# Strassen trunk on one core: weight blocks of 2 to 4, sums of squares in PSUM, softmax scale on ScalarE, and biases and silus issued once their operand is written

## The chip, the core and the metric

One core of a Trainium2 chip runs the whole kernel as one program. The metric is device time in microseconds; the time before is the median of three runs. The profile is one further execution of the same program.

The engines are named as in the profile: PE is the matrix engine (PEld its weight loads), DVE the vector engine, ACT the scalar (activation) engine, POOL the GpSimd engine, and SP the engine that issues nearly all DMAs. In the traces of this kernel each engine takes its instructions in the order of the program, and one that waits for another engine's semaphore holds up what stands behind it.

## The reference

One inference step of a two-layer trunk on 640 tokens (128 context tokens, 512 latent tokens) with 2048 features, in float32. Each layer is: RMS norm with a modulation, one wide input projection, two mixers side by side, a SiLU gate, an output projection, and a gated residual add.

```
even layer:  windowed attention with sinks   ||  gated linear attention (GLA)
odd layer:   neighbourhood attention (8 heads) ||  spatial gating (gMLP)
y = concat(mixer1, mixer2) * silu(gate)        # gate: part of the input projection
x = x + G * (y @ w_out)                        # G: gated residual, one per token group
final: rms_norm(x)
```

The modulation has its own matrix-vector products (the `ada` weights). The outputs are the tokens of both groups and the keys, values and states for the caches.

## The kernel before, in words

**Matmuls.** Activations lie in SBUF with features on the partitions and the 640 tokens along the free axis, in two halves of 320 (`HT`). A float32 product is made of three fast products: each operand is split into a high part, rounded to `fp32r`, and a low part, the rest. Of `high*high + high*low + low*high` each 128 x 128 weight block costs three matmuls of 320 columns (322 where two more columns carry the bias of the modulation's shift). Activations are `acth` and `actl`, weights are `whi` and `wlo`.

**Weight blocks.** A weight is loaded from DRAM by SP, ACT copies it to `whi` (a rounding copy), and POOL subtracts, `wlo = raw - whi`. Both go into a ring of 2560 columns (`RING`), that is 20 blocks of 128. In the plain products a split takes 4 blocks (512 columns) at once. A PE product frees its block in the ring (`wdone`) when the last matmul has been issued.

**Strassen pairs.** Most products of two output chunks c1, c2 with the two token halves go through `spair`: seven products instead of eight, called A11, A12, S1, S2, S4, S3, A22 for the weights that they use. Each product is made of 8 blocks (`ALL`, 31 such pairs) or 6 (`NS`, layer 0's output projection). A, the weight of the pair, has four quarters, called pieces 0 to 3 (A11, A12, A21, A22; quarters 0 to 2 in `rs`, quarter 3 in `adas`), and the sums S1 to S4 are made by four DVE instructions of 1024 columns, into piece 4 (`wraw`) or in place:

```
add1: wraw = q2 + q3     (S1)      add2: q2 = wraw - q0    (S2)
add3: q1 = q1 - q2       (S4)      add4: wraw = q3 - q2    (S3)
```

The activation sums that S1, S2 and A22 meet are `eh`/`el` (the first six blocks) and `fh`/`fl` (blocks 7 and 8). A split takes two blocks (256 columns), four splits a product, 28 a pair. The order of products is A11, A12, S1, S2, S4, S3, A22; in the first pair of a run of pairs A22 comes before S3. The next pair's quarters 0 and 1 are loaded after S4's splits, and quarters 2 and 3 at the end of the pair's list.

**The order of the work.** The program is written out by hand-made planning. The class `Pace` keeps a model of each engine's time; `tick` is called between matmuls (every second block) and issues, in program order, the work that the model takes to be due: the loads and splits of weights (`wpump`, which lets them run ahead by `lags`), the tasks of the mixers (generators that yield until an operand is ready), and a low-priority task for the `ada` products. What is issued early on an engine whose operand is late blocks that engine's queue.

**Evacuations.** When a projection's product is done, `lin` (projections) or `gate` (gates) brings it out of PSUM: DVE multiplies by the RMS factor `rstd` (PSUM to SBUF), ACT copies the two bias columns (`bc`), then ACT adds the bias (`lin`) or applies a silu with that bias (`gate`), and for most gates DVE multiplies the silu into the mixer's output `y`. All of these are issued in one go when PE's product has been issued. Where both halves come at once (`kpair`), DVE copies the bias and the multiplication is a task of its own (`late`). After it, `then` starts what depends on the result (a head, a transposition).

**Other places that the change touches.** `out_evac` makes the residual add of the output projection and the sums of squares for the next norm: ACT squares, then POOL (layer 0) or DVE (layer 1) adds to `ssq` in SBUF. `na_head` is a head of the neighbourhood attention: five blocks of scores, softmax (`soft1`, `soft2`), transposes, and products with the values `vk`; in the first and the last latent block one of the two value tiles has only 64 rows, and that matmul runs on half the partitions. `soft2` divides by the softmax sum, on ACT in the attention with sinks and on DVE in the neighbourhood attention.

Almost every operation is recorded through one helper, so line L218 stands for all of DVE, ACT and POOL, L447 for matmuls, L452 for transposes, and L484 for DMAs; the tile names tell them apart.

Of the kernel before, what the change touches and what calls it, by code (L numbers as in the profile page):

```python
# [35 lines left out]
NY, NZ, STAY = 8, 6, 10  # L36
OFF = 4
# [17 lines left out]
class Pace:  # L55
# [10 lines left out]
    COST = {"v": (0.07, 1 / 960), "a": (0.095, 0.84 / 1000), "g": (0.04, 2.35 / 1000)}  # L66
# [178 lines left out]
class Trunk:  # L245
# [9 lines left out]
    def __init__(self, tc, d, es):  # L255
# [6 lines left out]
        self.tasks = []  # L262
# [6 lines left out]
        self.cut = HT  # L269
# [37 lines left out]
        self.ident = self.P([128, 128], "ident")  # L307
# [94 lines left out]
    def widen(self, cs):  # L402

        yield from self.wait("r11", *(f"evac{c}" for c in cs))
        self.close_arena()
# [63 lines left out]
    rooms, calms, lags = (0.5, 1.5, 1.5), (3.0, 3.0), (3.0, 3.0, 2.0, 1.5, 1.0)  # L469
# [180 lines left out]
    def steps(self, c1, c2):  # L650

        names = lambda *x: [(c1, f) for f in x]
        if self.count[c1] == ALL:
            return names("A11", "A12", "S1", "S2", "S4", *(("A22", "S3") if c1 in self.opens else ("S3", "A22")))
        return [*names("A11"), (c1, PLAIN, 0), *names("A12", "S1", "S2", "S4"), (c2, PLAIN, 0), *names("S3", "A22")]

    def strassen_jobs(self, c1, c2, last, unit):
        ns, J = self.count[c1], self.jobs
        n, sub = 128 * ns, 2 if ns == ALL else ns // 2
# [10 lines left out]
        def load(i, c):  # L670
            if last is not None or ns != ALL:
                names = ()
            else:
                names = ("K", "H") if i else ("I", "J", "L")
            four = lambda x: x.rearrange("p (g r) c -> p g r c", r=4)
# [3 lines left out]
                    (piece(i + q, a, b), four(self.chunks[c][0])[:, JT[a] // 4 : JT[a] // 4 + (b - a) // 2, 2 * q : 2 * q + 2, :])  # L679
                    for q in range(2)  # L680
                    for a, b in ((0, 4), (4, ns))
                ],
                names,
# [3 lines left out]
        if last is None:  # L687
            J += [load(0, c1), load(2, c2)]
        else:
            J.insert(last[0], load(0, c1))  # L690
            J.insert(last[1] + 1, load(2, c2))
# [3 lines left out]
        if ns == ALL:  # L695
            after = {("A12", 3): [add1], ("S1", 1): [add2], ("S2", 1): [add3], ("S4", 1): [add4]}
        else:
            after = {("A12", 1): [add1, add2], ("S1", 1): [add3], ("S2", 1): [add4]}
        for c, f, *r in self.steps(c1, c2):
# [3 lines left out]
            for q in range(ns // sub):  # L703
                J.append(("split", (c1, f, q), lambda i=at[f], q=q: piece(i, sub * q, sub * q + sub), sub, 128, at[f] == 4))
                J += after.get((f, q), [])
            if f == "S4":
                done = len(J)
        return done, len(J)
# [27 lines left out]
    def wpump(self, force=False):  # L736
# [20 lines left out]
        lag = self.lags[min(sum(b - a for a, b in self.live.values()) // 512, 4)]  # L757
# [209 lines left out]
    def spair(self, c1, c2):  # L967
# [7 lines left out]
        sub = 2 if ns == ALL else ns // 2  # L975
# [31 lines left out]
        def product(b, view, f, x):  # L1007
            st = first(b)
            for i in range(ns):
                hi, lo = self.wget((c1, f, i // sub))  # L1010
                three(view(b), hi[:, i % sub, :], lo[:, i % sub, :], x(i), st and i == 0, i == ns - 1)
                if i % 2:
                    self.tick()
                if i % sub == sub - 1:
                    self.wdone((c1, f, i // sub))
# [239 lines left out]
    def lin(self, dst, scale=1.0, perm=False, then=None):  # L1255
# [3 lines left out]

        def evac(pa, pb):  # L1260
            M = dst.shape[0]
            lat = dst[:, NCTX:T].rearrange("p (g r c) -> p r g c", r=8, c=8) if perm else None
            if pa is not None:
                bc = box["bc"] = self.s("bc", 2)
# [7 lines left out]
                nc.scalar.activation(bc[:M], pa[:M, 0:2], AF.Copy, scale=scale)  # L1272
                nc.scalar.activation(dst[:, 0:NCTX], dst[:, 0:NCTX], AF.Identity, bias=bc[:M, 0:1], scale=scale)
            if pb is not None:
# [5 lines left out]
                nc.scalar.activation(dst[:, NCTX:T], dst[:, NCTX:T], AF.Identity, bias=bc[:M, 1:2], scale=scale)  # L1280
                if then:
                    then()

        return evac


    def gate(self, y, ring):
# [7 lines left out]
        def evac(pa, pb):  # L1295
# [9 lines left out]
            if pa is not None:  # L1305
                bc = box["bc"] = self.s("bc", 2)
                g = box["g"] = y if ring is None else ring.next()
                nc.vector.tensor_tensor(g[:, 0:HT], pa[:, 2 : 2 + HT], self.rstd[:, 0:HT], ALU.mult)
                nc.scalar.activation(bc, pa[:, 0:2], AF.Copy)
                self.act(g[:, 0:NCTX], g[:, 0:NCTX], AF.Silu, bias=bc[:, 0:1])  # L1310
                self.act(g[:, NCTX:HT], g[:, NCTX:HT], AF.Silu, bias=bc[:, 1:2])
                if ring:
                    nc.vector.tensor_tensor(y[:, 0:HT], y[:, 0:HT], g[:, 0:HT], ALU.mult)
            if pb is not None:
                bc, g = box["bc"], box["g"]
                nc.vector.tensor_tensor(g[:, HT:T], pb[:, 0:HT], self.rstd[:, HT:T], ALU.mult)
                self.act(g[:, HT:T], g[:, HT:T], AF.Silu, bias=bc[:, 1:2])
                if ring:
                    nc.vector.tensor_tensor(y[:, HT:T], y[:, HT:T], g[:, HT:T], ALU.mult)
# [1735 lines left out]
```

## Time and profile before

| | |
|---|---|
| median of three runs | 2063.18 us (2063.1 to 2065.52) |
| the profiled execution | 2068.56 us, its span 2066.8 us |
| mean granted clock of PE | 0.995 |
| PE busy | 2026.2 us, 98% of the span |
| DVE, ACT, POOL busy | 67%, 54%, 67% |
| DMA | 344.21 MB, mean 167 GB/s |

The stages by time, in us from the start of the span: 0 to 150 the first modulation and the first norm; 150 to 850 the even layer's projections with both mixers beside them; 850 to 1060 its gates' end and output projection; 1060 to 1310 the odd layer's gMLP projections; 1310 to 1650 the neighbourhood attention beside its projections; 1650 to 1850 the gates of the odd layer; 1850 to 2030 its output projection; then the final norm.

How to read it: a share of busy time says which engine could be the bound, not whether its stream has holes. Ends of matmuls are modelled in the profile, so a hole shorter than about a matmul's drain does not show as idle time. Counting matmuls in a window, and looking at starts, does show it. Timelines give the start, the length, the engine, the line and the operation, then the idle time in front and what ended it. Lines of groups give the count, the busy time, the mean of one in ns, and the idle time in front.

### The profile page before, as it was taken

How to read it: one execution, taken by the hardware profiler on the slowest of the kernel's cores; microseconds unless marked ns; L12 is line 12 of the kernel's file. 1: busy time of each engine (PE TensorE's matmuls, PEld its weight loads, DVE VectorE, ACT ScalarE, POOL GpSimd, SP SyncE). 2: the span in 40 equal slices, each digit the busy share in tenths (PEclk: the TensorE clock that was granted, in tenths of full speed). 3: DMA queues.
4: the chain of work that ended last, by engine and by line, in shares of the span. 5: the costliest groups of instructions: out<-in, count | busy, mean ns of one | idle time of the engine just before them, and what ended most of it. 6: DMA issues, size and time to landing. Idle time of an engine off the chain costs nothing.

```text
span 2066.8 us, 41426 instructions
## 1 busy us (share of the span) xinstructions
PE 2026.2 (98%) x14255; PEld 1978.7 (96%) x14255; DVE 1374.5 (67%) x3182; ACT 1109.7 (54%) x2758; POOL 1382.8 (67%) x1408
## 2 busy tenths in 40 slices
PE   8999999999999999999999999999999999999997
PEld 6899999999999999999999999999999999999996
DVE  4556678576667655888687777666676555577555
ACT  5445455444665565544565545555555655555543
POOL 4544455446455445888566978776866688968994
PEclk9999999999999999999999999999999999999999
DMA  9955433346466444677534344434434344265437
GB/s 382 393 200 162 128 111 106 120 128 206 142 205 209 148 156 155 198 241 221 204 127 133 121 155 151 128 118 138 142 115 132 99 154 131 85 211 184 141 102 280
DMA packets 234324, 344.21 MB, mean 167 GB/s; under 512 B 22048, under 2 KB 139648, under 8 KB 234112
## 3 DMA queue, kind: packets, MB, share of 16 engines
q1 hardware_dynamic: 232912, 340.38, 50.5%
q8 instruction: 112, 1.84, 0.4%
q10 hardware_dynamic: 1200, 1.17, 0.2%
q14 instruction: 100, 0.82, 0.1%
HBM read 304.99 MB, written 33.85 MB: 164 GB/s over the span
## 4 chain that ended last, share of the span: by engine, by line
PE 79%; DMA 8%; DVE 4%; issue 3%; POOL 3%; ACT 2%; SPq 1%; DVEq 0%; POOLq 0%; ACTq 0%
PE bank L447 77%; POOL wlo L218 2%; PE bank L452 2%; DVE bank L218 1%; DMA raw<-ada_s 1%; DMA more<-ada 1%; DMA Y<-xT 1%; DMA wraw<-w_even 1%; DVE adas L218 1%; SPq L484 1%; DMA actl<-bl_dram 1%; DVE arena L218 1%; ACT whi L218 1%; DMA adas<-ada_g 1%; DMA arena<-yT_dram 1%
## 5 line engine op out<-in xcount | busy, mean ns | idle before, releaser
L447 PE MATMUL bank<-acth,whi 128*128 128x320 f32 (+3 forms) x3072 | 942.5, 319 | 5.8 <-DVE YB L218 1.9
L447 PE MATMUL bank<-acth,wlo 128*128 128x320 f32 (+3 forms) x3072 | 915.9, 310 | 1.4 <-POOL wlo L218 1.4
L447 PE MATMUL bank<-actl,whi 128*128 128x320 f32 (+3 forms) x3072 | 915.6, 310 | 0.5 <-DMA actl<-bl_dram 0.5
L218 POOL TENSOR_TENSOR wlo<-wraw,whi 128x256 fp32r<-128x256 f32 (+2 forms) x508 | 558.7, 1117 | 487.4 <-ACT whi L218 407.6
L447 PEld LDWEIGHTS bank<-acth,whi 128*128 128x128 f32 (+1 forms) x3072 | 569.1, 188 | 15.6 <-issue 3.7
L447 PEld LDWEIGHTS bank<-actl,whi 128*128 128x128 f32 (+1 forms) x3072 | 569.4, 188 | 2.5 <-DMA actl<-bl_dram 0.7
L447 PEld LDWEIGHTS bank<-acth,wlo 128*128 128x128 f32 (+1 forms) x3072 | 568.1, 188 | 2.7 <-POOL wlo L218 2.5
L218 POOL TENSOR_TENSOR wlo<-rs,whi 128x256 fp32r<-128x256 f32 (+1 forms) x556 | 478.9, 893 | 59.5 <-ACT whi L218 55.6
L218 ACT ACTIVATE whi<-wraw 128x256 fp32r<-128x256 f32 (+2 forms) x518 | 253.9, 516 | 152.8 <-PE bank L447 88.8
L218 ACT ACTIVATE whi<-rs 128x256 fp32r<-128x256 f32 (+1 forms) x556 | 209.5, 421 | 70.0 <-PE bank L447 25.8
L447 PE MATMUL bank<-eh,wlo 128*128 128x322 f32 (+1 forms) x666 | 209.2, 314 | 3.5 <-POOL wlo L218 3.3
L447 PE MATMUL bank<-eh,whi 128*128 128x322 f32 (+1 forms) x666 | 209.2, 314 | 0.8 <-ACT whi L218 0.8
L447 PE MATMUL bank<-el,whi 128*128 128x322 f32 (+1 forms) x666 | 206.7, 310 | 0.0
L447 PEld LDWEIGHTS bank<-eh,wlo 128*128 128x128 f32 x666 | 125.7, 189 | 8.6 <-POOL wlo L218 8.2
L447 PEld LDWEIGHTS bank<-eh,whi 128*128 128x128 f32 x666 | 125.7, 189 | 1.1 <-ACT whi L218 1.0
L447 PEld LDWEIGHTS bank<-el,whi 128*128 128x128 f32 x666 | 125.7, 189 | 0.0
L218 DVE CUSTOM_DVE_ANT_0 adas<-adas,bank,part 128x512 bf16<-128x512 f32 x156 | 116.1, 744 | 10.7 <-DMA adas<-ada 7.5
L218 POOL TENSOR_TENSOR prod<-adas,mixrow 128x512 f32<-128x512 f32 x69 | 89.6, 1308 | 32.5 <-ACT prod L218 17.6
L218 DVE TENSOR_TENSOR bank<-bank,sums 128x320 f32<-128x320 f32 (+1 forms) x148 | 70.3, 493 | 61.3 <-PE bank L447 52.3
L218 ACT ACTIVATE bc<-bank 128x2 f32<-128x2 f32 (+1 forms) x91 | 15.6, 171 | 156.9 <-DVE adas L218 58.1
L218 POOL TENSOR_TENSOR wlo<-adas,whi 128x256 fp32r<-128x256 f32 x124 | 90.7, 760 | 11.3 <-ACT whi L218 9.9
L218 DVE TENSOR_TENSOR wraw<-rs,adas 128x1024 f32<-128x1024 f32 x31 | 45.2, 1458 | 62.4 <-DMA adas<-w_out 21.4
(277 smaller groups left out, 3099.3 us busy)
## 6 DMA issues: line engine op xcount, KB each, us to landing
wraw<-w_even SPq DMA_DIRECT2D x176, 256.0 KB, 3.3
rs<-w_odd SPq DMA_DIRECT2D x150, 256.0 KB, 3.5
adas<-ada SPq DMA_DIRECT2D x128, 256.0 KB, 3.9
adas<-ada_g SPq DMA_DIRECT2D x64, 256.0 KB, 3.6
rs<-w_out SPq DMA_DIRECT2D x60, 256.0 KB, 4.0
adas<-w_odd SPq DMA_DIRECT2D x50, 256.0 KB, 3.5
Y<-ada SPq DMA_DIRECT2D x24, 512.0 KB, 7.9
more<-ada SPq DMA_DIRECT2D x24, 512.0 KB, 8.2
```

Source lines behind the costliest of these rows:

```text
L218: return f(*args, **kw)
L447: self.nc.tensor.matmul(out, lhsT, rhs, start=start, stop=stop, **kw)
L452: self.nc.tensor.transpose(out, in_, self.ident[:k, :k])
L484: self.nc.sync.dma_start(out, in_)
```

## The change

It does five things, and shifts constants of the planner with them.

1. **Blocks.** In pairs of 8 blocks, A11, A12, S3 and A22 are split in blocks of 4, and S1, S2 and S4 in blocks of 2, 3 and 3 (17 splits a pair); pairs of 6 keep blocks of 3. The four quarters have a load each, put in the list right behind the last use of the quarter before, and A22 comes before S3 except in the last pair of a run.
2. **Sums of squares.** Layer 1 gathers them in two PSUM banks and copies them to `ssq` by ACT at the end; layer 0's last two squares are issued together.
3. **Scale.** `soft2` runs on ACT in both attentions.
4. **Full rows.** The last 64 keys of a neighbourhood head go to a tile `vend` of their own with the other 64 rows set to zero once, as for the first 64 keys in `vk`; so each value matmul has 128 rows.
5. **Deferral.** Where an evacuation takes one half at a time, the bias copy goes to DVE, and the bias or silu is put in a list (`later`). `settle`, called by `tick`, issues the head of the list once the model has its operand written; the multiplication of a gate is put in the list in turn, and so is `then`. `unused` holds an evacuation while its buffer still has such work open.

```diff
+CUTS = dict(dict.fromkeys(("A11", "A12", "S3", "A22"), (4, 4)), **dict.fromkeys(("S1", "S2", "S4"), (2, 3, 3)))
-    COST = {"v": (0.07, 1 / 960), "a": (0.095, 0.84 / 1000), "g": (0.04, 2.35 / 1000)}
+    COST = {"v": (0.07, 1 / 960), "a": (0.095, 0.84 / 1000), "g": (0.15, 2.15 / 1000)}
-    rooms, calms, lags = (0.5, 1.5, 1.5), ...
+    rooms, calms, lags = (0.5, 0.5, 1.5), ...
     def tick(self, n=1):
         self.dmas()
+        self.settle()
...
-            return names("A11", "A12", "S1", "S2", "S4", *(("A22", "S3") if c1 in self.opens else ("S3", "A22")))
+            return names("A11", "A12", "S1", "S2", "S4", *(("S3", "A22") if c1 in self.ends else ("A22", "S3")))
...
-        lag = self.lags[...]
+        lag = ((6.0, 6.0, 6.0, 3.0, 1.0) if self.quiet else self.lags)[...]
...
+    def later(self, f, *aps):
+        self.rests.append((f, aps))
+
+    def settle(self, force=False):
+        while self.rests and (force or self.left(*self.rests[0][1]) <= 0.05):
+            self.rests.pop(0)[0]()
...
     # gate, first half
                 nc.vector.tensor_tensor(g[:, 0:HT], pa[:, 2 : 2 + HT], self.rstd[:, 0:HT], ALU.mult)
-                nc.scalar.activation(bc, pa[:, 0:2], AF.Copy)
-                self.act(g[:, 0:NCTX], g[:, 0:NCTX], AF.Silu, bias=bc[:, 0:1])
-                self.act(g[:, NCTX:HT], g[:, NCTX:HT], AF.Silu, bias=bc[:, 1:2])
-                if ring:
-                    nc.vector.tensor_tensor(y[:, 0:HT], y[:, 0:HT], g[:, 0:HT], ALU.mult)
+                nc.vector.tensor_copy(bc, pa[:, 0:2])
+                def rest():
+                    self.act(g[:, 0:NCTX], g[:, 0:NCTX], AF.Silu, bias=bc[:, 0:1])
+                    self.act(g[:, NCTX:HT], g[:, NCTX:HT], AF.Silu, bias=bc[:, 1:2])
+                    if ring:
+                        self.later(lambda: nc.vector.tensor_tensor(y[:, 0:HT], y[:, 0:HT], g[:, 0:HT], ALU.mult), g[:, 0:HT])
+                self.later(rest, g[:, 0:HT])
...
     # soft2
-        if sink:
-            nc.scalar.activation(p, p, AF.Copy, scale=den)
-        else:
-            nc.vector.tensor_scalar(p, p, den, None, ALU.mult)
+        nc.scalar.activation(p, p, AF.Copy, scale=den)
...
     # out_evac, late
+            acc = self.ssqb[half][:, :HT] if l else self.ssq[:, c]
-                (nc.vector if l else nc.gpsimd).tensor_tensor(self.ssq[:, c], self.ssq[:, c], s, ALU.add)
+                (nc.vector if l else nc.gpsimd).tensor_tensor(acc, acc, s, ALU.add)
+            if l and i >= 2 * KT - 10:
+                nc.scalar.activation(self.ssq[:, c], acc, AF.Copy)
...
     # na_head, values
-                r = slice(64 * (j == 4), 64 if j == 0 else 128)
-                c = 512 if j in (0, 4) else 128 * j
-                self.mm(o, vk[r, c : c + 128], x[r, 128 + 128 * i : 256 + 128 * i], start=False, stop=i == 1)
+                v = self.vend if j == 4 else vk[:, 128 * (j or 4) : 128 * (j or 4) + 128]
+                self.mm(o, v, x[:, 128 + 128 * i : 256 + 128 * i], start=False, stop=i == 1)
```

The second handover also gets one more free tile (`D`) to load into.

More of the change, by code (lines that the diff above doesn't have):

```diff
@@ L702, in strassen_jobs @@
                 continue
[L703 to L708, printed above, removed]
+            for q, (k, m) in enumerate(self.blocks_of(ns, f)):
+                J.append(("split", (c1, f, q), lambda i=at[f], k=k, m=m: piece(i, k, k + m), m, 128, at[f] == 4))
+                for x in after.get((f, k + m), []):
+                    J.append(x)
+                    if x in ends:
+                        free[ends[x]] = len(J)
+                if k + m == ns and f in ("S4", "A22"):
+                    free[1 if f == "S4" else 3] = len(J)
+        return free
     def open_su(self, pool, n):
@@ L1008, in product @@
             st = first(b)
[L1009 to L1015, printed above, removed]
+            for q, (k, m) in enumerate(self.blocks_of(ns, f)):
+                hi, lo = self.wget((c1, f, q))
+                for i in range(k, k + m):
+                    three(view(b), hi[:, i - k, :], lo[:, i - k, :], x(i), st and i == 0, i == ns - 1)
+                    if i % 2:
+                        self.tick()
+                self.wdone((c1, f, q))
         def plain(key, a, b):
@@ L1279, in evac, with unused, gate @@
                     nc.vector.tensor_tensor(dst[:, HT:T], pb[:M, 0:HT], self.rstd[:M, HT:T], ALU.mult)
-                nc.scalar.activation(dst[:, NCTX:T], dst[:, NCTX:T], AF.Identity, bias=bc[:M, 1:2], scale=scale)
-                if then:
-                    then()
-        return evac
-    def gate(self, y, ring):
+                if both:
+                    rest(slice(NCTX, T), 1, then)()
+                else:
+                    self.later(rest(slice(NCTX, T), 1, then), dst[:, NCTX:T])
+        return evac
+    def later(self, f, *aps):
+        self.rests.append((f, aps))
+    def unused(self, x):
+        n, a, b = self.pace.span(x)
+        met = lambda: any(m == n and c < b and a < e for _, aps in self.rests for m, c, e in map(self.pace.span, aps))
+        while met():
+            self.now += 0.4
+            self.stall += 0.4
+            self.tick(4)
+    def settle(self, force=False):
+        while self.rests and (force or self.left(*self.rests[0][1]) <= 0.05):
+            self.rests.pop(0)[0]()
+    def gate(self, y, ring, then=None):
         nc = self.nc
@@ L2123, in late @@
             yield from self.calm(1.0, "a")
+            half = i % 2
+            if l and i < 2:
+                b = self.sm()
+                self.held.add(self.banks.index(b))
+                self.ssqb[half] = b
+            acc = self.ssqb[half][:, :HT] if l else self.ssq[:, c]
             if i < 2:
[L2125 removed]
+                nc.scalar.activation(acc, y[:, c], AF.Square)
             else:
@@ L2472, in evac @@
                     self.need(*pre)
-                    box["f"] = self.gate(y() if callable(y) else y, L[ring] if ring else None)
+                    box["f"] = self.gate(y() if callable(y) else y, L[ring] if ring else None, then)
                 last = box["f"](pa, pb)
-                if pb is not None and then:
+                if pa is not None and pb is not None and then:
                     assert last is None
```

108 lines of the change are left out of this document (70 added, 38 removed).

## The prediction

> **What bounds the kernel.** First the page's head and its first part.
>
> ```profile
> span 2066.8 us, 41426 instructions
> ...
> PE 2026.2 (98%) x14255; PEld 1978.7 (96%) x14255; DVE 1374.5 (67%) x3182; ACT 1109.7 (54%) x2758; POOL 1382.8 (67%) x1408
> ```
>
> TensorE is the bound, and the change leaves the number of matmuls alone, so all it can win is time in which the matmul stream runs slower than it could. A busy PE does not show that (ends of matmuls are modelled), so I went on to the windows, cut by stage, and counted matmuls. Columns: length, then busy time with the count for PE, PEld, DVE, ACT and POOL, granted clock, DMA share, GB/s.
>
> ```profile
> 150.00:500.00 350.00, 350.00 (x2417) 346.62 (x2416) 238.56 (x424) 181.96 (x370) 171.28 (x123) 1.00 0.43 134
> ...
> 850.00:1000.00 150.00, 149.82 (x1022) 149.56 (x1021) 130.31 (x297) 64.26 (x140) 127.18 (x116) 1.00 0.66 208
> 1000.00:1100.00 100.00, 96.98 (x638) 94.87 (x637) 69.72 (x147) 61.57 (x134) 54.78 (x43) 0.98 0.53 178
> ...
> 1310.00:1650.00 340.00, 339.47 (x2343) 333.53 (x2342) 228.35 (x698) 195.20 (x590) 239.18 (x306) 1.00 0.40 123
> 1650.00:1850.00 200.00, 195.75 (x1291) 191.40 (x1289) 110.42 (x153) 107.27 (x287) 170.24 (x190) 0.99 0.45 146
> 1850.00:2030.00 180.00, 178.65 (x1195) 176.46 (x1194) 113.39 (x162) 93.78 (x245) 162.35 (x183) 1.00 0.46 148
> ```
>
> 850 to 1000 is clean: 150/1022 = 0.1468 us per matmul. At that rate the 1291 matmuls of 1650 to 1850 (the gates of layer 1) need 189.5 us, so 10.5 us are lost; 1850 to 2030 (the last output projection) loses 180 - 1195 x 0.1468 = 4.6 us; 1000 to 1100 loses 6.3 us. The early projections (150 to 500: 0.1448 us each) lose nothing. Next, whom PE and its weight load wait for (whole span; 900 to 2030):
>
> ```profile
> PE bank L447 <- POOL wlo L218: 6.1, 15, 0.5
> ...
> PE bank L447 <- ACT bc L218: 1.6, 1, 1.6
> ```
> ```profile
> PEld bank L447 <- POOL wlo L218: 12.9, 25, 0.8
> ```
>
> It is the low half of a weight block, `wlo`, 25 times. In 1650 to 2030 these waits stand at the eh and fh matmuls, never at acth (form view: column 3 is the idle before):
>
> ```profile
> L447 PE MATMUL bank<-acth,wlo 128*128 128x320 f32 x384 | 113.7, 310 | 0.0
> ...
> L447 PE MATMUL bank<-eh,wlo 128*128 128x322 f32 x112 | 36.6, 327 | 2.0 <-POOL wlo L218 1.8
> L447 PE MATMUL bank<-eh,wlo 128*128 128x320 f32 x108 | 34.1, 316 | 1.0 <-POOL wlo L218 1.0
> ```
>
> eh belongs to the products S1, S2 and A22; S1 and S2 need sums of weights that DVE must form first. So not POOL's rate but a late start is to blame. The chain of waits shows the worst place, and ACT's timeline why:
>
> ```profile
> 1677.76 3.51 POOL wlo L218 x5
> ...
> 1681.30 1.75 DVE wraw L218
> ...
> 1683.12 4.12 issue
> ...
> ...
> 1689.73 18.33 PE bank L447 x112
> ```
> ```profile
> 1684.41 0.17 ACT L218 ACTIVATE bc<-bank 128x2 f32<-128x2 f32 x1 [6.40 <-DVE adas L218]
> 1684.61 0.75 ACT L218 ACTIVATE adas<-adas,bc 128x128 f32<-128x128 f32 x2
> 1686.33 0.56 ACT L218 ACTIVATE adas<-adas,bc 128x320 f32<-128x320 f32 x1 [0.96 <-DVE adas L218]
> 1686.79 0.40 ACT L218 ACTIVATE whi<-wraw 128x256 fp32r<-128x256 f32 x1
> ```
>
> The sum (DVE wraw) is ready at 1683.05. The split of its first block starts only at 1686.79: in ACT's queue it stands behind a bias copy and silus that wait for DVE, 3.7 us. That is most of the 4.12 "issue" of the chain. A sum can also be late itself, because one operand, quarter 3 (A22's), is loaded late. The queue of loads, then DVE, at a later pair:
>
> ```profile
> 1967.38 0.37 SPq L484 DMA_DIRECT2D adas<-w_out  x1
> ```
> ```profile
> 1974.01 1.23 DVE L218 TENSOR_TENSOR wraw<-rs,adas 128x1024 f32<-128x1024 f32 x1 [7.95 <-DMA adas<-w_out]
> ```
>
> DVE stood 7.95 us for a load issued when A22, the pair's last product, had been split.
>
> **The change part by part.**
>
> *Deferred biases and silus, bias copies on DVE.* On ACT goes the wait, not the work:
>
> ```profile
> L218 ACT ACTIVATE bc<-bank 128x2 f32<-128x2 f32 x90 | 15.4, 171 | 153.4 <-DVE adas L218 58.1 <-DVE arena L218 43.7 <-DVE Y L218 42.1
> ```
> ```profile
> L218 DVE COPY bc<-bank 128x2 f32<-128x2 f32 x4 | 0.6, 148 | 0.0
> ```
>
> ACT idles 153.4 us in front of 90 copies. Moved to DVE they cost 90 x 0.148 = 13.3 us, beside a PE stream that DVE does not bound (110.42 of 200 busy); if that cover were gone, the same 13.3 us. Behind the waiting ACT instructions stand the splits, and PE waits for those. The deferred work is polled between matmuls, so a head or a tail of a branch starts later by up to a polling step, two matmul triples, 0.9 us; what waits for it are heads and gate products, which PE does not wait for in the table above.
>
> *Loads by quarter, and A22 ahead of S3 except in a run's last pair.* Quarters 0 and 2 load when the sum has used them up; quarter 3 one product earlier: 24 matmuls x 0.1468 = 3.5 us, of 7.95. Same bytes, same number of DMAs on SP, which now stand ahead of the spills of gated tiles there: 0.37 us of SP each, eight a pair of 24.7 us (168 matmuls), so a spill waits some 3 us, and no tile's next use showed as a wait of PE. What is late next is the remaining 4.4 us of that worst wait, behind which DVE's other work also moves up.
>
> *Blocks of 4 (A11, A12, S3, A22) and 2, 3, 3 (S1, S2, S4).* A pair of 8 blocks a product goes from 28 splits to 17. Durations:
>
> ```profile
> L218 POOL TENSOR_TENSOR wlo<-rs,whi 128x256 fp32r<-128x256 f32 x496 | 410.2, 860 | 55.6 <-ACT whi L218 53.0 <-PE bank L447 2.0 <-DVE Y L218 0.2
> L218 POOL TENSOR_TENSOR wlo<-wraw,whi 128x512 fp32r<-128x512 f32 x232 | 316.4, 1369 | 361.5 <-ACT whi L218 295.4 <-PE bank L447 28.7 <-ACT bc L218 9.1
> ...
> L218 POOL TENSOR_TENSOR wlo<-rs,whi 128x384 fp32r<-128x384 f32 x60 | 68.7, 1164 | 3.8 <-ACT whi L218 2.6 <-PE bank L447 1.2
> ```
> ```profile
> L218 ACT ACTIVATE whi<-rs 128x256 fp32r<-128x256 f32 x496 | 178.9, 409 | 49.9 <-PE bank L447 22.0 <-issue 12.6 <-DVE rs L218 9.8
> L218 ACT ACTIVATE whi<-wraw 128x512 fp32r<-128x512 f32 x242 | 150.0, 624 | 86.4 <-PE bank L447 67.7 <-DMA wraw<-w_out 7.2 <-issue 5.8
> ```
>
> POOL: 28 x 0.860 = 24.1 us against 8 x 1.369 + 3 x 0.860 + 6 x 1.164 = 20.5 us a pair, 15% less on an engine busy 162.35 of 180 us in the last projection. The price is latency: an opening block of 4 takes 0.624 + 1.369 = 1.99 us instead of 0.409 + 0.860 = 1.27, so a PE that waits for one waits 0.72 us more. S1 and S2, where it waits today, still open with 2.
>
> *Sums of squares in PSUM (layer 1).*
>
> ```profile
> L218 DVE TENSOR_TENSOR Y<-Y 128x320 f32<-128x320 f32 x24 | 20.7, 861 | 5.8 <-ACT Y L218 5.8
> L218 DVE TENSOR_TENSOR bank<-bank,sums 128x320 f32<-128x320 f32 x24 | 11.2, 490 | 13.3 <-PE bank L447 13.3
> ```
>
> 24 x (0.861 - 0.490) = 8.9 us off DVE, two copies on ACT; all under PE, counted in the last projection's recovery. Two of the small banks are held meanwhile; no wait for such a bank stands in that stage, so nothing is put down.
>
> *Scale on ScalarE (neighbourhood attention).* What goes from DVE, and what the other attention pays on ACT for the same form:
>
> ```profile
> L218 DVE TENSOR_SCALAR Y<-Y,den 128x384 f32<-128x384 f32 x16 | 9.4, 584 | 0.6
> ```
> ```profile
> L218 ACT ACTIVATE arena<-arena,den 128x384 f32<-128x384 f32 x16 | 9.8, 613 | 1.0 <-DVE den L218 0.6
> ```
>
> 40 scalings at no more than 0.613 us put up to 24.5 us on ACT, busy 195 of 340 there: hidden by PE, which runs 339.47 of 340. Zero; without that cover, 0.03 us in each of 40 chains. The planner's new constants, rooms and lags and the one more buffer (D) only shift order: bounded by the largest wait of PE on anything but `wlo` after the start, the 1.6 us on `bc`, either way; zero.
>
> *Full rows in the neighbourhood attention.* The matmuls on half the rows go. PE's timeline, a block with one and a block without:
>
> ```profile
> 1330.47 0.90 PE L447 MATMUL bank<-Y,adas 64*128 64x128 f32 x4
> 1331.21 0.71 PE L447 MATMUL bank<-Y 128*128 128x192 f32 x4
> ```
> ```profile
> 1334.97 0.61 PE L447 MATMUL bank<-Y,adas 128*128 128x128 f32 x4
> 1335.34 0.39 PE L447 MATMUL bank<-acth,whi 128*128 128x320 f32 x1
> ```
>
> From the group's start to the next: 0.74 against 0.37 us, two blocks a head, 8 heads: 16 x 0.37 = 5.9 us, directly on the bound. The Trainium skill (TensorE: Matmul & The Clock Gate, "LDWEIGHTS") says a weight load's time goes by columns and that the rows do not matter; by that this part would win nothing and the sum be 5.9 us less. The skill's TensorEngine Tiling (Array Packing), "Key Properties", says that changing the tiling mode drains TensorE, and that is what the rows look like. I go by the rows.
>
> **The sum.** Of the gates' 10.5 us I take 7 back: part is two more columns a matmul and the handover at its end, and part is this clock dip, which follows the stalls before 1689.7:
>
> ```profile
> 1689.50:1693.50 4.00, 3.77 (x15) 3.78 (x16) 2.95 (x3) 1.93 (x7) 4.00 (x6) 0.57 0.43 131
> ```
>
> 15 matmuls in 4 us instead of 27, so 1.8 us, at a granted clock of 0.57. The Trainium skill (TensorE: Matmul & The Clock Gate, "What's actually happening") throttles after an idle window of about 3.4 us; PE had no such gap here, so by it the dip would not go with the stalls, and the sum would be 1.8 us less. Of the projection's 4.6 I take 3, of the 6.3 around the second handover 1 (its pairs keep blocks of 3). With 5.9 that is 16.9 us. New waits at opening blocks of 4: none shows today, at most one in each of 31 pairs (22 us); I take six, 4.3 us, nearer the empty row. Net -12.6 us: the profiled execution would go from 2068.56 (span 2066.8 and 1.76 around it) to 2056; that execution stands 0.26% above the median 2063.18, which becomes 2050.6.
>
> **Rivals.** *The waits only move* (little change): the earlier load still lands late, splits stay late, and only the full rows count, less 4.3 for new waits: -1.6, 2061.6. For it: 4.4 of 7.95 us remain. Against: the 3.7 us behind the silus goes whatever the load does.
>
> *Long blocks stall PE* (slower): every pair pays 0.72 us for an opening block of 4, 31 x 0.72 = 22.3 against 16.9: +5.4, 2068.6. It decides from 29 pairs if the gains come whole, from 14 if only the rows' 5.9 do. For it: the ring of 2560 columns holds five long blocks. Against: four of them cover 48 matmuls, 7 us.
>
> *Half rows cost nothing by themselves* (the first rule): -6.7, 2056.5.
>
> **How the numbers follow.** The forecast 0.62 (2040 to 2058: down to all 15.1 us of the last two stages and the rows, some 21 us with a little of the 6.3), rows without effect 0.08, waits only move 0.14, long blocks 0.16. The forecast and the third rival are faster: 0.70; the first is within 0.2% (4.1 us, about what three runs from 2063.1 to 2065.52 can tell): 0.14; slower 0.16. The range runs from 2040 to 2067, leaving the slower case out.
>
> **What would show it.** Right: no 64-row matmuls; ACT's idle before bias copies gone; DVE's wait for adas loads at about half; `wlo` waits of PE under 5; some 1310 to 1325 matmuls in a 200 us window of the gates; 17 splits a pair. Wrong: `wlo` waits at acth matmuls, or PE waiting for banks that a deferred bias still holds.

## The result and the profile after

The changed kernel takes 2054.49 us, median of four runs (2053.29 to 2055.43), against 2064.35 us for the kernel before on the same chip (four runs, 2063.1 to 2067.85): 9.9 us less, a ratio of 0.9944, 95% interval 0.9926 to 0.9962. The forecast was 2050.6 us. The profiled execution took 2053.88 us against 2068.56 before, 14.7 us less; 4.2 us of that is that the profiled execution before stood above its median.

The page's head of the changed kernel, to be read against the one in the prediction:

```profile
span 2052.1 us, 40329 instructions
...
PE 2012.5 (98%) x14255; PEld 1975.3 (96%) x14255; DVE 1364.1 (66%) x3191; ACT 1093.2 (53%) x2414; POOL 1356.6 (66%) x1088
```

The matmuls are the same 14255. POOL has 320 instructions fewer, ACT 344, and still TensorE is busy 98% of the span: the shares show nothing of what happened. The windows do (same stages and columns as in the prediction):

```profile
150.00:500.00 350.00, 350.00 (x2419) 346.71 (x2418) 234.18 (x424) 182.04 (x360) 177.04 (x127) 1.00 0.42 132
850.00:1000.00 150.00, 150.00 (x1025) 150.00 (x1024) 118.36 (x242) 65.06 (x140) 128.52 (x119) 1.00 0.57 182
1000.00:1100.00 100.00, 95.59 (x636) 93.15 (x635) 62.18 (x129) 58.96 (x127) 50.19 (x38) 1.00 0.50 173
1100.00:1310.00 210.00, 206.91 (x1411) 205.68 (x1410) 159.48 (x371) 99.13 (x215) 163.58 (x131) 0.99 0.40 124
1310.00:1650.00 340.00, 340.00 (x2389) 338.53 (x2389) 220.53 (x699) 201.89 (x495) 229.81 (x193) 1.00 0.42 131
1650.00:1850.00 200.00, 200.00 (x1359) 199.87 (x1358) 136.82 (x222) 104.38 (x222) 169.45 (x128) 1.00 0.47 154
1850.00:2030.00 180.00, 179.68 (x1208) 178.83 (x1207) 98.29 (x157) 84.13 (x176) 143.37 (x114) 1.00 0.53 173
```

And the stretch from 1100 to 1310 of the kernel before, which the prediction did not show:

```profile
1100.00:1310.00 210.00, 209.71 (x1449) 209.22 (x1448) 161.11 (x406) 113.64 (x322) 176.22 (x220) 1.00 0.43 136
```

The gates went from 1291 to 1359 matmuls in 200 us, the neighbourhood attention from 2343 to 2389 in 340. But 1100 to 1310, the start of the odd layer, fell from 1449 to 1411, and 1000 to 1100 gained nothing.

Since the stages slide against fixed windows, I compared from here on by matmul number: the time between the starts of matmul n and matmul m in two traces, of which each holds all 14255. The table gives the difference in us to the profiled execution of the changed kernel; a plus is slower than that one. The numbers are the first matmuls of the stretches, which end at matmul 7500, 8500, 11500, 12750, 14000 and the last; what lies between them is under "other". Each stretch holds the same shapes of matmuls in all traces, apart from a few in the neighbourhood attention. "e11_again" is the changed kernel once more, unedited.

```
                   0    7500   9250  11750  13050  14000
                 early  odd    neigh.       last          other  total
kernel           part   start  attn.  gates  proj.  end
before           -1.1   -5.5   +6.5   +8.7   +3.7   +1.2   +1.1  +14.6
e1_half          +5.9   +0.0   +5.4   +0.1   +0.0   -0.6   +0.8  +11.6
e2_nodefer       -0.7   -1.3   +1.6   +2.8   +0.7   -0.6   -0.1   +2.4
e3_oldloads      +1.1   -4.9   -0.0   +0.5   +0.1   -0.6   -0.6   -4.5
e4_twos          +3.1   -0.2   -0.1   +1.8   +0.6   +0.6   -0.0   +5.9
e5_p5_old        +4.7   -4.1   +2.4   +8.3   +0.2   -0.6   -0.5  +10.4
e6_old_twos_ssq  +3.4   -1.1   -0.6   +2.8   +4.7   +5.8   +0.3  +15.3
e7_p5_old_twos   +4.1   -1.6   +0.1  +10.8   +0.1   -0.6   -0.5  +12.5
e8_old_q         +4.1   -8.8   -0.3   +0.1   +2.0   -0.6   -0.2   -3.6
e9_sbufssq       +5.3   -1.2   +0.6   +1.5   +0.0   -0.6   +0.0   +5.6
e10_crow         +7.8   -2.8   -0.1   +0.1   +0.8   -0.6   +0.8   +6.1
e11_again        +3.6   -1.4   +0.0   +2.6   +0.8   -0.4   +0.7   +5.9
e12_best         +5.8   -8.8   +2.1   +0.6   +0.6   -0.6   +0.2   +0.1
```

The row of e11_again says how far a single profile can be read: the same program differs from itself by 3.6 us in the early part, 2.6 in the gates, 1.4 at the odd layer's start. Differences below that are not explained here. The early part of the first trace lies lower than that of all later runs but one, so totals are not compared, only stages; what the early part does hold is told under the costs. Of the kernel before there is one trace.

What PE waited for, whole span, in the changed kernel (us in total, times, longest):

```profile
PE bank L454 <- ACT adas L219: 2.7, 1, 2.7
...
PE bank L449 <- POOL wlo L219: 0.7, 2, 0.3
```

and its weight load, from 900 to 2030 us:

```profile
PEld bank L449 <- POOL wlo L219: 1.7, 4, 0.6
```

The waits for `wlo` are nearly gone (6.1 us in 15 and 12.9 in 25 before; in the repeat 1.7 us in 4 and 3.5 in 7), and a wait on `adas`, an ACT tile, has grown in front of a transpose (L454): 2.7 us in one piece at the start of the odd layer, where the kernel before waited 0.3.

### The profile page after: what moved, and what is told of

Its sections match the earlier page's. It is cut to its first block, busy times and chain, and to the rows that moved or that the text cites. A ratio compares the mean times of both kernels' runs of the same rounds, so it can differ in the third digit from the quotient of the medians.

```text
span 2052.1 us, 40329 instructions
## 1 busy us (share of the span) xinstructions
PE 2012.5 (98%) x14255; PEld 1975.3 (96%) x14255; DVE 1364.1 (66%) x3191; ACT 1093.2 (53%) x2414; POOL 1356.6 (66%) x1088
## 4 chain that ended last, share of the span: by engine, by line
PE 82%; DMA 9%; DVE 4%; ACT 2%; issue 1%; POOL 1%; SPq 0%; DVEq 0%; POOLq 0%; ACTq 0%
PE bank L449 80%; PE bank L454 2%; DMA more<-ada 1%; DMA Y<-xT 1%; DMA Y<-ada 1%; DMA wraw<-w_out 1%; DVE bank L219 1%; POOL wlo L219 1%; DMA wraw<-w_even 1%; DMA adas<-ada 1%; DMA raw<-ada_s 1%; DMA adas<-ada_g 1%; DVE adas L219 1%; DVE arena L219 1%; ACT whi L219 1%
## 5 line engine op out<-in xcount | busy, mean ns | idle before, releaser
L219 POOL TENSOR_TENSOR wlo<-wraw,whi 128x512 fp32r<-128x512 f32 (+2 forms) x415 | 535.5, 1301 | 401.9 <-ACT whi L219 347.4
L219 POOL TENSOR_TENSOR wlo<-rs,whi 128x384 fp32r<-128x384 f32 (+2 forms) x370 | 456.2, 1258 | 114.3 <-ACT whi L219 83.0
L219 ACT ACTIVATE whi<-wraw 128x512 fp32r<-128x512 f32 (+2 forms) x425 | 245.4, 586 | 146.6 <-PE bank L449 71.3
L219 ACT ACTIVATE whi<-rs 128x384 fp32r<-128x384 f32 (+2 forms) x370 | 189.7, 535 | 92.4 <-PE bank L449 46.7
L219 POOL TENSOR_TENSOR prod<-adas,mixrow 128x512 f32<-128x512 f32 x87 | 113.2, 1311 | 48.6 <-ACT prod L219 34.3
L219 DVE CUSTOM_DVE_ANT_0 adas<-adas,bank,part 128x512 bf16<-128x512 f32 x146 | 108.7, 744 | 23.4 <-DMA adas<-ada 20.5
L219 POOL TENSOR_TENSOR wlo<-adas,whi 128x512 fp32r<-128x512 f32 x62 | 81.3, 1317 | 35.4 <-ACT whi L219 26.9
L219 ACT ACTIVATE sums<-bank 128x320 f32<-128x320 f32 (+1 forms) x111 | 48.3, 435 | 99.7 <-PE bank L449 97.8
L219 DVE CUSTOM_DVE_ANT_0 old<-rawx,bank,partg 128x256 bf16<-128x256 f32 x140 | 66.8, 477 | 27.4 <-DMA rawx<-ada_g 24.2
```

The costliest lines, as they stand in the source:

```text
L219: return f(*args, **kw)
```

## The experiments

Each ran beside the kernel before on the same chip; the ratios are to that. Medians of the kernel before: 2065.48 us beside e1 to e4, 2066.82 beside e5 to e8, 2067.84 beside e9 to e12.

### Half rows again

```diff
-                v = self.vend if j == 4 else vk[:, 128 * (j or 4) : 128 * (j or 4) + 128]
-                self.mm(o, v, x[:, 128 + 128 * i : 256 + 128 * i], start=False, stop=i == 1)
+                r = slice(64 * (j == 4), 64 if j == 0 else 128)
+                v = self.vend[r, :] if j == 4 else vk[r, 128 * (j or 4) : 128 * (j or 4) + 128]
+                self.mm(o, v, x[r, 128 + 128 * i : 256 + 128 * i], start=False, stop=i == 1)
```

> The changed kernel with the value matmuls of the neighbourhood attention on half rows again (the zero rows stay, unused). Theory, half-row matmuls cost PE time by themselves: 5.9 us come back, 2054.5 to about 2060.4, all of it between the start and the end of the neighbourhood attention. Rival, the rows do not matter and that stage gained by the earlier loads and the longer blocks: no more than 1 us, 2054 to 2055.5.

2064.17 us (10 runs), ratio 0.9988 (0.9976 to 1.0001). In the neighbourhood attention +5.4 us, in gates and projection nothing. Its groups of matmuls there have the 64 rows again (line engine op out<-in, array, shape xcount | busy, mean ns | idle before):

```profile
L449 PE MATMUL bank<-Y,adas 64*128 64x128 f32 x16 | 3.9, 323 | 0.0
L449 PE MATMUL bank<-Y,vend 64*128 64x128 f32 x14 | 3.4, 323 | 0.0
```

The mean of one, 323 ns, tells nothing of a price of 5 us; the starts do. PE's timeline of the changed kernel at such a block:

```profile
1343.16 0.39 PE L449 MATMUL bank<-Y,adas 128*128 128x128 f32 x2
1343.38 0.39 PE L449 MATMUL bank<-Y,vend 128*128 128x128 f32 x2
1343.52 0.39 PE L449 MATMUL bank<-acth,whi 128*128 128x320 f32 x1
```

And the same block in e1:

```profile
1349.29 0.39 PE L449 MATMUL bank<-Y,adas 128*128 128x128 f32 x2
1349.61 0.48 PE L449 MATMUL bank<-Y,vend 64*128 64x128 f32 x2
1350.02 0.41 PE L449 MATMUL bank<-acth,whi 128*128 128x320 f32 x1
```

Four value matmuls take 1343.52 - 1343.16 = 0.36 us from the group's start to the next, with half rows 1350.02 - 1349.29 = 0.73. So the prediction's term (5.9) is shown, at 5.4 to 6.5. The weight loads themselves are not slower (e1, count, busy, mean ns, idle before):

```profile
L449 PEld LDWEIGHTS bank<-Y,adas 128*128 128x128 f32 x110 | 15.4, 191 | 1.0
L449 PEld LDWEIGHTS bank<-Y,vend 64*128 64x128 f32 x14 | 2.1, 185 | 0.8
```

The Trainium skill (TensorE: Matmul & The Clock Gate, "LDWEIGHTS") says that the time of a weight load goes by columns and not by rows; the trace agrees, 185 ns against 191. It does not follow from it that half rows cost nothing, as the prediction's third rival had it: the loss is around the load. In the changed kernel the load for the last pair of the block starts at 1343.27, 0.11 us before its matmuls and beside the pair before; in e1 it starts at 1349.60, with its matmuls, and the load behind it at 1350.02. That fits the drain at each change of the mode which the skill's TensorEngine Tiling (Array Packing), "Key Properties", states. The median gains 1.3 us over the kernel before where the changed kernel gains 9.9, that is 8.6 less, 3 more than the stage accounts for; in the trace the early part is 5.9 us longer, where the unedited repeat is 3.6.

### One part undone at a time: deferral, loads, blocks, sums

```diff
 e2_nodefer   def later:    -        self.rests.append((f, aps))
                            +        f()
 e3_oldloads  steps:        -  *(("S3", "A22") if c1 in self.ends else ("A22", "S3"))
                            +  *(("S3", "A22") if c1 not in self.opens else ("A22", "S3"))
              strassen_jobs:-        return free
                            +        return {0: free[1], 1: free[1], 2: len(J), 3: len(J)}
 e4_twos                    +CUTS = dict.fromkeys(("A11", "A12", "S3", "A22", "S1", "S2", "S4"), (2, 2, 2, 2))
              (adds of S1, S2, S4 after 4 blocks instead of 5)
 e9_sbufssq   out_evac:     -  acc = self.ssqb[half][:, :HT] if l else self.ssq[:, c]
                            +  acc = self.ssq[:, c]        (and no copies at the end)
```

> The changed kernel with every deferred bias, silu and gate multiplication issued at once, as before the change; bias copies stay on DVE. Theory, splits stood behind silus in ACT's queue: the gates lose 5 to 8 us again by waits for wlo, the output projection, which has no biases, loses nothing: about 2061. Rival, the earlier loads and the order of the products carried the gain of the gates: within 1.5 us of 2054.5. A third reading, that deferral also costs at the odd layer's start (a stall of 2.9 us at a transposition of a projection behind a deferred bias): that stall goes, and the net is 2057 to 2058.

> The changed kernel with the loads of the quarters where they were (0 and 1 after S4, 2 and 3 at the pair's end) and the order of S3 and A22 as before the change. Theory, the sums waited for quarter 3: DVE's wait for adas loads returns to 20 us and more in the last output projection, and 3 to 5 us of PE time with it: about 2058.5. Rival, with the queues free the load has time enough: within 1.5 us of 2054.5.

> The changed kernel with all blocks of 2 (28 splits a pair). Theory, POOL and ACT were never short of rate, only late: POOL busy goes up by some 3 us a pair, some 90 us in all, and the time stays within 1.5 us of 2054.5. Rival, the relief of 15% on POOL carried the gain of the last two stages: 5 us or more come back, above 2059.

> The changed kernel with only the sums of squares back in SBUF. Undone together with loads and blocks they gave back 4.7 us in the last output projection, where the loads alone gave 0.1 and the blocks 0.6. Theory, the additions of two SBUF operands on DVE are what makes the splits late there: 3 to 4 us return. Rival, slack again, loads and blocks cover it: under 1 us.

| | median us (runs) | ratio, 95% |
|---|---|---|
| e2_nodefer | 2056.82 (5) | 0.9961 (0.9944 to 0.9978) |
| e3_oldloads | 2051.26 (4) | 0.9935 (0.9918 to 0.9951) |
| e4_twos | 2057.91 (5) | 0.9957 (0.9940 to 0.9975) |
| e9_sbufssq | 2058.18 (5) | 0.9952 (0.9935 to 0.9968) |

No single one gives the gates or the projection back: at most 2.8 of 8.7 and 0.7 of 3.7, about what the repeat does by itself (2.6 and 0.8). The theories put first for e2, e3 and e9 are refuted; e4 by its median (2057.91) lies between its two. Yet e3 and e9 did on DVE what they were meant to. With the old loads (e3 also takes the order of S3 and A22 back) DVE waits for quarter 3 again in the last projection (1845 to 2020); first the kernel before, then the changed kernel, then e3:

```profile
L218 DVE TENSOR_TENSOR wraw<-rs,adas 128x1024 f32<-128x1024 f32 x6 | 8.4, 1394 | 26.8 <-DMA adas<-w_out 21.4 <-POOL wlo L218 5.5
```
```profile
L219 DVE TENSOR_TENSOR wraw<-rs,adas 128x1024 f32<-128x1024 f32 x6 | 9.1, 1518 | 4.2 <-POOL wlo L219 3.4 <-DMA adas<-w_out 0.6
```
```profile
L219 DVE TENSOR_TENSOR wraw<-rs,adas 128x1024 f32<-128x1024 f32 x6 | 11.7, 1942 | 18.0 <-DMA adas<-w_out 18.0
```

DVE's wait for the load goes from 0.6 to 18.0 us and PE loses 0.1 us. And with the sums of squares in SBUF again, DVE's adds cost more than twice as much; the changed kernel, then e9:

```profile
L219 DVE TENSOR_TENSOR bank<-bank,Y 128x320 f32<-128x320 f32 x22 | 10.8, 493 | 6.2 <-ACT Y L219 6.2
```
```profile
L219 DVE TENSOR_TENSOR Y<-Y 128x320 f32<-128x320 f32 x24 | 26.2, 1095 | 2.8 <-ACT Y L219 2.8
```

15.4 us more on DVE, and again nothing on PE. Late loads and late adds are both there on DVE, and neither costs PE anything in this stretch alone. So I formed another theory: the parts cover for one another, and each leaves enough slack for one of the others to be missing.

### Several parts undone together

```diff
 e5_p5_old        e2 + e3, and the bias copies on ACT again (where both halves come at once, as before)
                  -                nc.vector.tensor_copy(bc, pa[:, 0:2])
                  +                nc.scalar.activation(bc, pa[:, 0:2], AF.Copy)
 e7_p5_old_twos   e5 + e4          (sums of squares stay in PSUM)
 e6_old_twos_ssq  e3 + e4 + e9     (deferral and copies on DVE stay)
```

> The changed kernel without part 5 (no deferral, bias copies on ACT) and with the loads and the order of products of before; blocks of 4 and 2, 3, 3, PSUM sums and full rows stay. Undone alone, deferral gave back 2.8 us in the gates and the loads 0.5. Theory of slack: each edit puts the sums and their splits some us earlier and a stall comes only where all slack is gone, so two undone together cost more than their sum, 5 to 8 us in the gates: about 2058. Rival, the blocks (1.8 alone) are what matters and the rest adds: 3 to 4 us in the gates.

> The changed kernel with the loads and the order of before, all blocks of 2, and the sums of squares in SBUF; deferral, bias copies on DVE and full rows stay. Theory of slack: deferral alone holds most of the gates' 8.7 us (at most 3 return), while in the last output projection, which has no biases, nothing of the change is left but the planner's constants, and its 3.7 us return: about 2055 with the odd layer's start freed of its 4.9. Rival, the planner's cost for POOL and its looser lags carry the projection: no more than 1.5 us return there.

> The changed kernel without part 5 and with the loads, the order and the blocks of 2 of before; PSUM sums, scale on ACT, full rows and the planner's constants stay. Theory of slack: all 8.7 us of the gates return, and of the projection's 3.7 what the PSUM sums do not hold. Rival, the planner's constants hold part of it: 5 us or less return in the gates.

| | median us (runs) | ratio, 95% | gates | last projection, end |
|---|---|---|---|---|
| e5_p5_old | 2062.13 (8) | 0.9977 (0.9959 to 0.9995) | +8.3 | +0.2, -0.6 |
| e6_old_twos_ssq | 2068.15 (8) | 1.0001 (0.9983 to 1.0020) | +2.8 | +4.7, +5.8 |
| e7_p5_old_twos | 2065.24 (8) | 0.9992 (0.9976 to 1.0007) | +10.8 | +0.1, -0.6 |

By their totals e5 and e6 missed what was expected (2058 and 2055 us); their stages in the gates came as the theory of slack had them. There neither the deferral (e2) nor the loads (e3) is missed alone, but without both, and with the bias copies on ACT, the loss is back (e5), and it is not back where of all these only part 5, the deferral and its copies, remains (e6). So part 5 by itself is enough. The weight load's wait in the gates (1660 to 1870; the kernel before 6.4 us in 13, the changed kernel none, its repeat 1.8 in 3), e5, e7 and e6 in turn, and the windows of e5 and e7:

```profile
PEld bank L449 <- POOL wlo L219: 7.5, 13, 1.3
```
```profile
PEld bank L449 <- POOL wlo L219: 7.6, 14, 1.0
```
```profile
PEld bank L449 <- POOL wlo L219: 2.8, 7, 0.8
```
```profile
1650.00:1850.00 200.00, 195.85 (x1305) 191.36 (x1303) 116.21 (x194) 100.71 (x227) 157.60 (x123) 1.00 0.46 149
```
```profile
1650.00:1850.00 200.00, 194.35 (x1287) 190.12 (x1286) 110.12 (x152) 107.70 (x289) 163.41 (x188) 0.99 0.44 143
```

e7's row is that of the kernel before almost to the matmul (1287 and 1291). In the last projection there are no silus, and there the slack is shown from both ends: the PSUM sums hold the time alone (e7, +0.1), and so do early loads with long blocks (e9, 0.0); without either, the loss is back (e6, +4.7). The +5.8 at e6's end, where the kernel before has +1.2, is a single stall of PE of 2.8 us behind a late `whi` split, with a clock dip; why it comes there stays open.

In the gates the other end is not shown. e5 and e7 undo two things of part 5, the deferral and the engine of the copies, and e2 undoes the deferral alone. So a single cause, the copies on DVE, would fit all five figures of the gates as well: they stay on DVE in e2, e3 and e6, where the time holds, and go back to ACT in e5 and e7, where it is lost. One trace speaks against it. What ACT waited for in front of all instructions that touch `bc`, 1660 to 1870, in the kernel before and in e2:

```profile
  DVE adas L218: 45.2, 24
  DVE bc L218: 1.8, 1
```
```profile
  DVE adas L219: 24.4, 12
  DVE bc L219: 21.6, 13
```

With the copies on DVE but nothing deferred ACT stands as long as before the change (46.0 and 47.0 us), and yet the weight load waits 2.7 us for `wlo` instead of 6.4. So the copies did not free ACT's queue; that the early loads hold the time in e2 is the likelier reading. The run that would settle it, e2 with the old loads, was not made.

### What the change costs: the start of the odd layer

The new wait of 2.7 us is a transpose that waits for `adas`, which ACT's bias writes. ACT's timeline of the changed kernel says what stood in front of it:

```profile
1125.33 0.39 ACT L219 ACTIVATE bank<-rawx 128x256 f32<-128x256 f32 x1 [2.26 <-DMA rawx<-crow_s]
1126.66 0.39 ACT L219 ACTIVATE bank<-rawx 128x256 f32<-128x256 f32 x1 [0.94 <-DMA rawx<-crow_s]
1126.98 0.61 ACT L219 ACTIVATE whi<-rs 128x512 fp32r<-128x512 f32 x1
1127.50 0.71 ACT L219 ACTIVATE adas<-adas,bc 128x512 f32<-128x512 f32 x1
```

ACT stands 2.26 + 0.94 us for a row being broadcast by DMA (`crow_s`), then does a weight split, and only then the bias. It is the same fault as in the gates before, an early issue in front of an urgent one, with a DMA as the late operand. e3 lowers this stage by 4.9 us (3.5 to the repeat). Three more runs ask which of DMA, loads and planner's lags it is:

```diff
 e8_old_q    e3, and the lags as before in all pairs
             -        lag = ((6.0, 6.0, 6.0, 3.0, 1.0) if self.quiet else self.lags)[...]
             +        lag = self.lags[...]
 e10_crow    the planner takes the 256-column rows of crow_s to land 3 us later
             -        rows = in_.name == SHIFTS
             +        rows = in_.name == SHIFTS or in_.name == "crow_s" and in_.shape[-1] == 256
 e11_again   nothing
 e12_best    e3, and the longer lags only after the last head's values
             -        lag = ((6.0, 6.0, 6.0, 3.0, 1.0) if self.quiet else self.lags)[...]
             +        lag = ((6.0, 6.0, 6.0, 3.0, 1.0) if self.quiet and "nh7" in self.flags else self.lags)[...]
```

> A version meant to be the fastest: the changed kernel with the loads and the order of before (which freed the odd layer's start of a 2.9 us stall behind a slow broadcast of the conditioning row), and the lags of splits in the quiet pairs as before the change (6, 6, 6, 3, 1 gone). If the splits issued early are what blocks DVE and ACT at the second handover (stalls of 1.1, 1.45 and 0.9 us of PE there), 2 to 3 us go beside the 4.9: 2048. If not, 2050, as with the loads alone.

> The changed kernel with one constant of the planner: the 256-column broadcasts of the conditioning row are taken to land 3 us later than before, so that ACT's copy of them is listed later. Theory, the 2.9 us stall of PE at 1125 us and the clock dip behind it come from ACT standing in its queue before that copy, with a deferred bias and a transposition behind it: 3 to 5 us go in the odd layer's start, nothing elsewhere but a drift of 1 us. Rival, the broadcast only shows what the loads delay: the stall moves to another wait and no more than 1 us goes.

> The changed kernel once more, unedited, on one chip with the next version: 0.994 to 0.996 of before, 2054 to 2057.

> The changed kernel with the loads and the order of products of before, and the looser lags of quiet pairs only after the last neighbourhood head (they cost 4 us at the second handover and gained 2 in the last output projection). If these add: 4.5 us from the loads, 4 from the lags, so 6 to 8 us under the changed kernel, 2046 to 2049; if the second projection's 2 us were drift, 2050.

| | median us (runs) | ratio, 95% | odd start, to e11 |
|---|---|---|---|
| e8_old_q | 2050.13 (4) | 0.9927 (0.9906 to 0.9949) | -7.4 |
| e10_crow | 2054.31 (4) | 0.9935 (0.9913 to 0.9958) | -1.4 |
| e11_again | 2058.10 (6) | 0.9945 (0.9928 to 0.9963) | 0 |
| e12_best | 2046.16 (6) | 0.9902 (0.9885 to 0.9919) | -7.4 |

e11 repeats the result: the ratio is 0.9945 after 0.9944. e10 shortens the wait on `adas` to 1.2 us (2.9 in the repeat), but the stage gains only 1.4 us on the repeat, as much as the two traces of one program differ by: the late row is at most a part of the cause. Old loads with the old lags there take all of it: the waits of PE from 1040 to 1300 us in e12,

```profile
PE bank L449 <- POOL wlo L219: 1.0, 1, 1.0
PE bank L449 <- ACT bc L219: 0.5, 1, 0.5
```

are all that is left, and the stage is 3.3 us faster than in the kernel before. How longer lags hurt shows at the second handover, in DVE's timeline of the changed kernel:

```profile
1056.96 0.48 DVE L219 TENSOR_TENSOR bank<-rs 128x320 f32<-128x320 f32 x1
1060.09 2.06 DVE L219 TENSOR_TENSOR wlo<-wraw,whi 128x512 fp32r<-128x512 f32 x1 [2.64 <-ACT whi L219]
1062.07 0.48 DVE L219 SCALAR_TENSOR_TENSOR arena<-rstd 128x320 f32<-128x320 f32 x1
```

A split that was issued early holds DVE for 2.64 us and then 2.06, and the norm's chain (`rstd`), which the whole next layer needs, starts right behind it. In e8 no split stands directly in front of that instruction, which waits 1.43 us for ACT's `rstd` instead, as it does in the kernel before (1.85). e3, with the longer lags still there, has the same 2.64 and 2.06 us on DVE as the changed kernel.

e12 beats both kernels: 11.9 us (0.58%) under the unedited change on the same chip and 21.7 us under the kernel before. Its profiled execution (2053.82 us) is its slowest, the other five lie from 2044.95 to 2046.89. That the longer lags are worth keeping after "nh7" fits the last projection (e8, without them, loses 2.0 us, e12 0.6, the repeat 0.8) and the medians (16.7 and 21.7 us under the kernel before on their chips), but the intervals of the two overlap, so it is not shown.

**The even layer pays too.** The early part holds a second cost, which the table shows only as scatter. From matmul 3868 to 6181 (500 to 850 us of the kernel before, the even layer's mixers) the ten traces with the deferral take 2.8 to 7.7 us longer than the kernel before (the changed kernel 2.8, its repeat 5.2); the three without it take 1.3 (e2), 1.4 (e5) and -0.9 (e7). What grew is the kind of wait that the odd layer's start shows, a transpose behind a bias on ACT, here of `arena`; the kernel before, then the changed kernel, 500 to 850 us:

```profile
PE bank L452 <- ACT arena L218: 0.9, 2, 0.7
```
```profile
PE bank L454 <- ACT arena L219: 3.7, 5, 1.7
```

From 495 to 865 us it is 2.8 to 5.2 us in the ten traces and 1.4 to 2.3 in the three. So the deferral that helps the gates costs some 3 to 5 us here. This and the odd layer's start are why the medians gain 9.9 us where rows, gates and last projection give some 15 to 19.

## Why the prediction was right, and where it was not

**Size.** -9.9 us by medians (forecast -12.6), inside the range, on the likeliest case's side.

**Full rows: -5.9 forecast, 5.4 to 6.5 measured.** Right, by the rows and against the rule.

**Gates: -7 forecast, 6.1 (the repeat) to 8.7 measured.** Right in size (the stretch has 1000 of the gates' matmuls; from 11750 to 13050 it is 6.3 to 9.6): few of the `wlo` waits of before are left, and there is no clock dip (granted clock 1.00 in the window). The window has 1359 matmuls, in the repeat 1336, where 1310 to 1325 were named; that sign was too low for the sum itself, in which 7 us are 48 matmuls at 0.1468, that is 1339. The reason was too simple. It named one cause, the splits behind ACT's waiting silus. Part 5, which was to take them away, is enough to keep the loss away (e6), but the loss stays away too where ACT waits as long as before (e2). Nor is ACT's idle gone. What ACT waited for in front of all instructions that touch `bc`, whole span (us, times), before and after:

```profile
  DVE adas L218: 87.5, 49
  DVE arena L218: 56.6, 35
  DVE Y L218: 51.6, 30
```
```profile
  DVE bc L219: 80.5, 58
  DVE adas L219: 28.1, 16
  DVE Y L219: 11.5, 5
```

195.7 us became 120.1 in these three rows: ACT now waits for the copy on DVE instead, 1.4 us a time, where the copy itself takes 0.15: the model takes the operand for written before DVE has come to it.

**Last projection: -3 forecast, 3.0 (to the repeat) to 3.7 measured.** Right in size. The late quarter 3, which the prediction named for it, is refuted as a cause by itself: e3 has 18.0 us of that wait on DVE and loses nothing. The wait, forecast at about half, fell from 21.4 us to 0.6. POOL is 12% less busy there (143.37 after 162.35), where 15% a pair was worked out; a single split of 256 columns from `rs` took 962 ns over the whole span where it had taken 860.

**New waits at opening blocks of 4: +4.3 forecast, none seen.** All waits of PE on `wlo` are 0.7 us, none longer than 0.3 (1.7 in the repeat, in front of eh matmuls). e4, without long blocks, is nowhere faster by more than 0.2 us.

**The failed step: loads, lags, constants and buffer "only shift order", zero within 1.6 us; and -1 at the second handover.** Measured at the handover and the odd layer's start: +4.1 to +5.5 us. The early loads (with the order of S3 and A22) are some 3.5 to 4.9 us of it (e3 to the repeat and to the first trace) and the longer lags in quiet stretches some 3.9 more (e8 to e3); with blocks of 2 beside them the old loads bring only 1.1 to 1.6 (e6, e7), what the repeat does by itself, so these do not add up either. My bound of 1.6 us was the largest wait that the trace before showed, but moved work makes waits that are not in that trace.

**A second failed step: deferral costs nothing, since PE does not wait for what waits for it.** In the even layer it does: transposes behind a deferred bias, 2.8 to 5.2 us there in the two traces of the changed kernel. These unforeseen costs, 8 to 9 us together, stand against the missing 4.3 us and gains a little above their forecasts, so the sum came nearer than its parts; that is luck.

**The rivals.** Waits that only move (2061.6) and long blocks that stall PE (2068.6) are refuted by the gates' and e4's rows, half rows without effect (2056.5) by e1. The first was half right in kind: the waits did move, though to other stages: the odd layer's start takes 4.1 to 5.5 us of a gain of some 15 to 19, and with the even layer it is about half.

**Left open.** The scale on ScalarE, POOL's cost constant, the rooms and the tile D were not run alone; between 1310 and 1650 ACT is 6.7 us busier and DVE 7.8 less, and PE runs 340.00 of 340. Why e10 keeps the stage's loss is not settled beyond the split that holds DVE. In the gates it is open whether the early loads or the copies on DVE hold the time without the deferral.

## What to carry to other kernels

When undoing one edit that removes a visible wait costs nothing, undo it together with the others before calling it worthless: several causes of the same lateness cover for one another, and each edit leaves slack in which another may be missing. Choose the combinations so that a single cause cannot fit them all. When an edit lets work be issued earlier, cost what stands behind it on each in-order queue at the next handover, where an early split or a late DMA in front of a norm or a transpose is paid in full. And before reading a stage difference of 1 to 3 us from a single profile, profile the same program twice.

## What the hardware showed that was not expected

The clock. At the odd layer's start PE idles 2.75 us in the first trace of the changed kernel, and a dip follows; in the repeat it idles 2.92 us, and none does (windows behind the stall, the granted clock third from the end; the first trace, then the repeat):

```profile
1128.50:1131.50 3.00, 3.00 (x14) 3.00 (x13) 2.17 (x9) 1.62 (x4) 1.82 (x3) 0.50 0.24 78
```
```profile
1131.70:1134.70 3.00, 2.83 (x20) 2.83 (x21) 1.75 (x9) 2.04 (x5) 2.74 (x3) 1.00 0.27 89
```

14 matmuls in 3 us against 20 (and 0.17 us of the second window still belong to the stall): the dip costs some 0.9 us more. The Trainium skill (TensorE: Matmul & The Clock Gate, "What's actually happening") puts the dip after an idle window of about 3.4 us that runs freely. That the longer of the two stalls is missed and the shorter hit agrees with a free window; but the dip after 2.75 us, and the one of the kernel before at 1689.5, after idle stretches of 0.76, 0.25 and 0.52 us, came without a gap of that length.

A DVE add of 128x320 from SBUF to SBUF, the sums of squares, took 1095 ns in e9's last projection and 1174 in e6's, where the same adds took 861 in the kernel before; adds of that size with one operand and the output in PSUM took 490 to 496 ns there in all of these. What sets the time of the slow ones was not tested.
